# A two-layer decoder trunk on one core: four operands laid out by the host instead of turned over by transposes

## The chip, the core and the metric

The kernel runs on one core of a Trainium2 chip. Its engines are TensorE (PE, with PEld for its weight loads), VectorE (DVE), ScalarE (ACT), GpSimd (POOL) and SyncE (SP), which only issues transfers; POOL and ACT issue transfers too. Matmuls write into eight banks of PSUM, each 128 partitions by 512 f32; everything else lives in SBUF. The metric is the device time of one execution in microseconds, the median of three runs. What the host does to lay out the inputs before the launch is not part of it.

## The reference

Two layers work on `x` of 512 positions by 1024. In each layer, with an rmsnorm ahead of and behind every sub-layer:

```
z = h @ w_in                               # split among three mixers
w = where(tril, sgu_w, 0)                  # sgu_w (4, 128, 128), indices h, t, s
s = einsum('hts,bnshd->bnthd', w, v) + sgu_b.T     # sgu_b (4, 128)
A = u * s                                  # spatial gating, chunks of 128
B = retention(...)                         # 6 heads of 64
C = forgetting_attention(...)              # 6 heads of 64
x += rmsnorm(concat(A, B, C) @ w_o)
g = h @ w_gate                             # 1024 -> 4096
conv = conv_b + sum_j shift(g, j) * conv_w[j]      # conv_w (3, 4096)
x += rmsnorm((gelu(conv) * (h @ w_up)) @ w_down)
x += rmsnorm((p[i] @ w_ple_proj) * sigmoid(rmsnorm(x) @ w_ple_gate))   # p[i] (512, 256)
```

All inputs are float32. `sgu_w`, `sgu_b`, `conv_w`, `conv_b` and `p` are the ones that the change touches.

## The kernel before, in words

**Data.** Large weights are laid out by the host (`packed`, L507) so that a transfer reads long rows. In the kernel they are split into a coarse part and a remainder (tiles in fp32r), and a product is a sum of products of parts. The 4096 columns of the feed-forward network are worked off in 32 blocks of 128. For one block `gate_up` (L1285) runs 84 matmuls of 128x128 by 128x256 (`alpha`, `beta`, `gamma` are their banks; `wsa`, `wsb`, `wg` are weights prepared by DVE and ACT from a loaded `graw`), and from block 4 on a share of the down projection (`dn`) stands between them. The gate half then goes through a convolution of three taps: ACT makes `cv` from `gs` with a tap and the bias as per-partition scalars, and DVE adds the two other taps. These scalars stand in `cw`, 128 partitions by 4 by 32.

**Stages.** For each layer: `mixers` (L965), `out_proj` (L1244), `ffn` (L1274), and the gated embedding of `p` at the layer's end, whose product `p @ w_ple_proj` is made much earlier (`embed_operands` from L1376, `embed`). The spatial gating is in `mixers` at L997: it waits for gate values `av`, and its results `oa` are turned over again into the concatenated operand by `cps` transposes. Attention's blocks are `pe` (the exponentials, on ACT), turned over by `tps`, then `fet`. `rr`, `rm` and `mix` belong to the retention's rotary and its products. The program's start (L1471 to L1512) runs 16 idle bf16 matmuls, then `embed_operands(0, (0,), True)`, that is, half of layer 0's embedding product, then the first chunk of `x` and its norm (`junk` is what ACT's squares write, `h` the normed chunk, `hps` its transposes).

**Where transposes stand that the change concerns.** `sgu_w[l]` is loaded with position t on the partitions into `sguw`, masked there by POOL, turned over by four `wtps` transposes into one bank, and copied by ACT to `wT`. `sgu_b[l]` is loaded as 4 rows into `sgub`, turned over (`sbps`), and copied by DVE to `bT`. `conv_w` and `conv_b` are loaded as 128 rows of 128 into `cpar`, turned over (`cpps`), and copied by DVE to `cw` (L1275 to L1281). `p[l]` is loaded in two halves into `pr` with positions on the partitions, turned over by eight `pps` transposes, and each bank is split by ACT and DVE to `pT`. This is done twice for layer 0 (once for each half of the output columns) and once for layer 1.

**What sets the order.** Nothing is issued where it is written. Class `Plan` (L51) records every operation with its tiles, and `issue` (L252, the call itself in L452) replays them by a list scheduler: each engine takes, of the operations whose inputs its cost model holds ready, the earliest in the program. An operation may start ahead of its place only by a window counted in operations (`AHEAD`, L62). A tile from a pool waits until one of the pool's buffers is free: `sguw`, `sgub`, `cpar`, `pr`, and the mixers' `rr`, `sq`, `oa`, as well as the network's `gs`, `us`, `cv`, are all tiles of one pool of twelve buffers of 128x512 (`wk`, L565). So an operation less in one place can shift others before and behind it. On the chip, each engine runs its own list in that fixed order and waits at its head. Since every instruction is issued in L452, all rows of the profile name that line, and an operation is known by its tiles.

Of the kernel before, what the change touches and what calls it, by code (L numbers as in the profile page):

```python
# [33 lines left out]
ALU = mybir.AluOpType  # L34
AX = mybir.AxisListType

P = 128
D = 1024
S = 512
NCH = 4  # L40
# [466 lines left out]
def packed(w):  # L507

    def turned(m):
        n = block(m.shape[-1])  # L510
        m = m.reshape(*m.shape[:-1], -1, n // 2, 2)
        return m.swapaxes(-1, -2).reshape(*m.shape[:-3], -1)

    def rows(m, order=None):

        m = turned(m).reshape(-1, P, m.shape[-1])
        return (m if order is None else m[list(order)]).transpose(1, 0, 2)

    def blocks(m):

        return m.reshape(KB, P, -1, P).transpose(2, 1, 0, 3).reshape(-1, P, KB * P)

    r = {}
    r["uv"] = [rows(m[:, C_U:C_U + 512]) for m in w["w_in"]]
    r["rv"] = [rows(m[:, C_RV:C_RV + 384]) for m in w["w_in"]]
    r["fv"] = [rows(m[:, C_FV:C_FV + 390]) for m in w["w_in"]]
    def pairs(g, u):
        g, u = (blocks(m).reshape(-1, P, 2, 512) for m in (g, u))
        return np.stack([u[:, :, 1], u[:, :, 0], g[:, :, 0], g[:, :, 1]], 2)

    r["rg"] = [blocks(m[:, C_RG + 2 * P:C_RG + 3 * P])[0] for m in w["w_in"]]
    r["fm"] = [pairs(*(np.concatenate([m[:, p[i]:p[i] + P] for p in PAIRS], 1) for i in range(2))) for m in w["w_in"]]
    r["gu"] = [pairs(g, u) for g, u in zip(w["w_gate"], w["w_up"])]
    r["dn"] = [turned(m).reshape(8, 4, P, 2, 512).transpose(0, 3, 2, 1, 4) for m in w["w_down"]]
    r["wo"] = [np.stack([rows(m[:, c:c + 512], O_ORDER) for c in (0, 512)]) for m in w["w_o"]]
    r["pg"] = [np.stack([rows(m[:, c:c + 512]) for c in (0, 512)]) for m in w["w_ple_gate"]]
    r["pe"] = [rows(m) for m in w["w_ple_proj"]]
    return {k: np.ascontiguousarray(np.stack(v)) for k, v in r.items()}


def body(ctx, tc, a, out):
    nc = tc.nc
    plan = Plan(tc)
# [18 lines left out]
    def bank(name="ps"):  # L562
        return ppt([P, 512], F32, tag="ps", name=name, bufs=8)

    def wk(name, shape=(P, 512), dt=F32):  # L565
        return kpt(list(shape), dt, tag="wk", name=name, bufs=12)
# [90 lines left out]
    def split(dst_hi, dst_lo, src):  # L657
        A.copy(dst_hi, src)
        V.tensor_tensor(out=dst_lo, in0=src, in1=dst_hi.bitcast(F32), op=ALU.subtract)
# [305 lines left out]
    def mixers(l, hT, uv, ready):  # L965
# [5 lines left out]
        wT = m2[:, 1536:2048]  # L971
# [24 lines left out]

        def gating():  # L997

            wn = wk("sguw")
            SY.dma_start(out=wn.rearrange("p (h s) -> p h s", h=4), in_=a["sgu_w"][l].rearrange("h t s -> t h s"))  # L1000
            G.affine_select(out=wn, in_=wn, pattern=[[0, 4], [-1, P]], compare_op=ALU.is_ge, fill=0.0, base=0, channel_multiplier=1)
            ps = bank("wtps")
            for h in range(4):
                T.transpose(ps[:, h * P:(h + 1) * P], wn[:, h * P:(h + 1) * P], ident)
            A.copy(wT, ps)
            sb = wk("sgub", (P, P))
            SY.dma_start(out=sb[0:4, :], in_=a["sgu_b"][l])
            ps = bank("sbps")
            T.transpose(ps[:, 0:4], sb[0:4, :], ident[0:4, 0:4])
            bT = small("bT", 4, bufs=2)  # L1010
            V.tensor_copy(bT, ps[:, 0:4])
            SY.dma_start(out=gv, in_=a["sgu_v_g"][l].rearrange("h d -> (h d)").unsqueeze(0).to_broadcast([P, 256]))
            ss = small("ss16", 16, bufs=1)
            for hf in range(2):
                sq = wk("sq")
                src = m4[:, 1024 + hf * 512:1024 + hf * 512 + 512]
                A.activation(sq, src, AF.Square, scale=0.125)
                V.tensor_reduce(out=ss[:, hf * 8:hf * 8 + 8], in_=sq.rearrange("p (g d) -> p g d", d=64), axis=AX.X, op=ALU.add)
            r16 = rstd([ss], 16)
            for c in range(NCH):  # L1020
                v3 = av[:, c, :].rearrange("p (h d) -> p h d", h=4)
                V.tensor_tensor(out=v3, in0=v3, in1=r16[:, c * 4:c * 4 + 4].unsqueeze(2).to_broadcast([P, 4, 64]), op=ALU.mult)
                V.tensor_tensor(out=av[:, c, :], in0=av[:, c, :], in1=gv, op=ALU.mult)
            oa = [wk("oa") for _ in range(2)]
            pss = [bank("sps") for _ in range(2)]
            with plan.together():
                for h in range(4):
                    T.matmul(pss[h // 2][:, h % 2 * 256:h % 2 * 256 + 256], lhsT=wT[:, h * P:(h + 1) * P], rhs=av[:, :, h * 64:h * 64 + 64], start=True, stop=True)
            for b, ps in enumerate(pss):
                ov = oa[b].rearrange("p (c s d) -> p c s d", c=NCH, s=2)  # L1030
                for i in range(2):
                    h, hs = 2 * b + i, slice(i * 256, i * 256 + 256)
                    V.scalar_tensor_tensor(
                        out=ov[:, :, i, :], in0=ps[:, hs].rearrange("p (c d) -> p c d", c=NCH), scalar=bT[:, h:h + 1],
                        in1=au[:, :, h * 64:h * 64 + 64], op0=ALU.add, op1=ALU.mult)
            for b in range(2):
                to_concat(cc, b, oa[b])
# [166 lines left out]
        for step in STEPS.split():  # L1204
            h = int(step[1]) if len(step) > 1 else 0
# [66 lines left out]
        return emb  # L1272

    def ffn(l, hs, emb, ready, x, new, g, nxt):  # L1274
        cpar = wk("cpar")  # L1275
        SY.dma_start(out=cpar[0:96, 0:P], in_=a["conv_w"][l].rearrange("j (b f) -> (j b) f", f=P))
        SY.dma_start(out=cpar[96:128, 0:P], in_=a["conv_b"][l].rearrange("(b f) -> b f", f=P))
        ps = bank("cpps")
        T.transpose(ps[:, 0:P], cpar[:, 0:P], ident)
        cw = wpt([P, 4, 32], F32, tag="cw", name="cw", bufs=1)  # L1280
        V.tensor_copy(cw, ps[:, 0:P].rearrange("p (j b) -> p j b", j=4))  # L1281
        facc = []
        acts = {}

# [91 lines left out]
    def embed_operands(l, halves=range(2), at_once=False):  # L1376

        pT = b8("pT", (2, 2, S), F32R)
        raw = b8("eraw", (2, D))
        us = {hf: b8("ehl", (2, 2, 512), F32R) for hf in halves}  # L1380

        def weights(k):
            for hf, u in us.items():
                cs = slice(hf * 512, hf * 512 + 512)
                SY.dma_start(out=raw[:, k, cs], in_=a["w_pe"][l][:, k, cs])

        weights(0)
        prs = []
        for c2 in range(2):
            pr = wk("pr")  # L1390
            prs.append(pr.rearrange("p (c n) -> p c n", c=2))
            SY.dma_start(out=prs[c2], in_=a["p"][l, 0, c2 * 256:c2 * 256 + 256, :].rearrange("(c p) n -> p c n", p=P))
            if not c2:
                weights(1)
        for c2, prv in enumerate(prs):
            for k in range(2):
                ps = bank("pps")
                for c in range(2):
                    T.transpose(ps[:, c * P:(c + 1) * P], prv[:, c, k * P:(k + 1) * P], ident)
                ts = slice(c2 * 256, c2 * 256 + 256)  # L1400
                split(pT[:, 0, k, ts], pT[:, 1, k, ts], ps[:, 0:256])
                if not c2:
                    for hf, u in us.items():
                        split(u[:, 0, k, :], u[:, 1, k, :], raw[:, k, hf * 512:hf * 512 + 512])
            if at_once:
                embed(l, pT, us, range(1, NCH) if c2 else range(1))
                plan.fence(not c2)
        return pT, us

    def embed(l, pT, us, chunks=range(NCH)):  # L1410

        for hf, u in us.items():
            cs = slice(hf * 512, hf * 512 + 512)
            e = b8("e", (NCH, 512))
            for c in chunks:
                ps = bank("eps")
                ts = slice(c * P, c * P + P)
                for k in range(2):
                    mm3(ps, lambda i: pT[:, i, k, ts], lambda i: u[:, i, k, :], k == 0, k == 1)
                A.copy(e[:, c, :], ps)  # L1420
                SY.dma_start(out=ed[l][:, c, cs], in_=e[:, c, :])
# [77 lines left out]
    parts = []  # L1499
# [16 lines left out]
    for l in range(DEPTH):  # L1516
# [17 lines left out]
    plan.issue()  # L1534


_INS = ["x", "p", "positions", "sgu_v_g", "sgu_w", "sgu_b", "fox_b_f", "conv_w", "conv_b", "mix_pre_g", "mix_post_g",
        "ffn_pre_g", "ffn_post_g", "ple_pre_g", "ple_post_g"]


# [17 lines left out]
```

## Time and profile before

| | us |
|---|---|
| median of three runs | 1526.82 (1526.79 to 1529.71) |
| the profiled execution | 1528.62 |
| span of its profile | 1526.9 |

The span is what the profile's clock covers, from the first to the last recorded instruction; the execution's own time is 1.7 us longer.

| engine | busy us | share of the span | instructions |
|---|---|---|---|
| PE | 1496.3 | 98% | 10554 |
| PEld | 1383.6 | 91% | 10554 |
| DVE | 1216.7 | 80% | 2036 |
| ACT | 888.9 | 58% | 1501 |
| POOL | 194.3 | 13% | 233 |

In a timeline, a row gives the start (us from the span's start), the time from the first start to the last end, the engine, the line, the operation, `out<-in` by the program's names, shapes and the number of instructions run together in the row; in brackets stands idle time ahead of it and what ended it. A row of the waits gives the engine's waiting tile, the one it waited for, the sum in us, how often, and the longest. A row of the groups gives the sum in us and the mean in ns, and behind the bar the idle time ahead. A row of the windows gives the stretch and its length, the busy us of PE, PEld, DVE, ACT and POOL with instructions in brackets, the granted clock of TensorE (1.00 is full speed), the share of the transfer engines and their GB/s.

### The profile page before, as it was taken

Reading aid. Unit: us, or ns where it says so; the run is one execution under the profiler, and the core shown is the slowest. Engines: PE = TensorE matmul, PEld = TensorE weight load, DVE = VectorE, ACT = ScalarE, POOL = GpSimd, SP = SyncE. Lnnn points to the kernel's source line nnn. Section 1 sums busy time; section 2 is a strip of 40 time slices with the busy share of each in tenths; the row PEclk is TensorE's granted clock in tenths of the full one; section 3 lists DMA queues with packets and bytes.
Section 4 is the critical chain, followed back from the end, with each engine's and each line's share of the span. In section 5 each row is a group of like instructions: output and inputs, shape, how many; then the busy total and the mean of one; then the engine's idle time right before and its main releaser. Section 6 shows DMA issues by size and latency. Waiting matters only on the chain.

```text
span 1526.9 us, 26942 instructions
## 1 busy us (share of the span) xinstructions
PE 1496.3 (98%) x10554; PEld 1383.6 (91%) x10554; DVE 1216.7 (80%) x2036; ACT 888.9 (58%) x1501; POOL 194.3 (13%) x233
## 2 busy tenths in 40 slices
PE   8999999999999999999999999999999999999997
PEld 6998888899999999998889887799999999999987
DVE  6888969978778777768797779799688778778685
ACT  8557647755555545545575565587655555455462
POOL 1111102111101111100120102121101011011010
PEclk9999999999999999999999999999999999999999
DMA  9445619735646646556573355295545565465541
GB/s 335 88 135 122 209 52 280 189 90 146 173 90 175 150 117 173 146 155 245 190 197 99 92 146 182 68 334 130 146 117 153 163 149 130 123 174 139 212 174 70
DMA packets 87879, 239.02 MB, mean 157 GB/s; under 512 B 10036, under 2 KB 18364, under 8 KB 87752
## 3 DMA queue, kind: packets, MB, share of 16 engines
q1 hardware_dynamic: 64856, 195.81, 37.6%
q0 software_dynamic: 22464, 40.90, 17.0%
q8 instruction: 83, 1.36, 0.4%
q10 hardware_dynamic: 432, 0.59, 0.1%
q14 instruction: 44, 0.36, 0.1%
HBM read 219.94 MB, written 17.33 MB: 155 GB/s over the span
## 4 chain that ended last, share of the span: by engine, by line
PE 74%; DVE 8%; DMA 5%; ACT 5%; issue 5%; POOL 1%; SPq 0%; POOLq 0%; DVEq 0%; ACTq 0%
PE beta L452 20%; PE dn L452 19%; PE ps L452 13%; PE gamma L452 11%; PE alpha L452 5%; DMA graw<-in_w_gu_dram 3%; DMA traw<-in_w_dn_dram 2%; PE wo L452 1%; ACT rr L452 1%; PE hps L452 1%; DVE cv L452 1%; PE tps L452 1%; PE ops L452 1%; ACT junk L452 1%; POOL y L452 1%
## 5 line engine op out<-in xcount | busy, mean ns | idle before, releaser
L452 PE MATMUL dn<-thl,act 128*128 128x512 f32 x1536 | 351.7, 380 | 0.0
L452 PEld LDWEIGHTS dn<-thl,act 128*128 128x128 f32 x1536 | 281.8, 189 | 35.0
L452 POOL DMA_DIRECT2D graw<-in_w_gu_dram x128 | 112.1, 908 | 733.4 <-DVE wg L452 232.0
L452 PE MATMUL ps<-thl,hT 128*128 128x512 f32 (+3 forms) x984 | 198.7, 358 | 2.5 <-ACT hT L452 2.4
L452 PEld LDWEIGHTS ps<-thl,hT 128*128 128x128 f32 x984 | 171.6, 189 | 19.5 <-ACT hT L452 2.9
L452 DVE TENSOR_TENSOR thl<-traw,thl 128x1024 fp32r<-128x1024 f32 (+3 forms) x124 | 141.8, 1152 | 13.4 <-ACT thl L452 13.3
L452 ACT CAST thl<-traw 128x1024 fp32r<-128x1024 f32 (+3 forms) x124 | 121.2, 995 | 21.2 <-PE dn L452 9.2
L452 PEld LDWEIGHTS beta<-hh,wu 128*128 128x128 f32 x936 | 123.2, 191 | 7.2 <-DVE us L452 1.4
L452 PE MATMUL beta<-hh,wu 128*128 128x256 f32 x936 | 126.2, 275 | 1.0 <-DVE us L452 0.9
L452 PE MATMUL beta<-hh,wsa 128*128 128x256 f32 x936 | 120.6, 277 | 6.1 <-ACT gs L452 3.2
L452 PE MATMUL gamma<-hhd,wsa 128*128 128x256 f32 x936 | 120.8, 277 | 0.9 <-ACT wsa L452 0.8
L452 PEld LDWEIGHTS beta<-hh,wsa 128*128 128x128 f32 x936 | 111.4, 192 | 9.2 <-ACT gs L452 4.4
L452 PE MATMUL beta<-hh,wsb 128*128 128x256 f32 x936 | 118.0, 276 | 0.1
L452 DVE TENSOR_TENSOR graw<-graw 128x512 f32<-128x512 f32 x156 | 106.7, 684 | 10.4 <-DMA graw<-in_w_gu_dram 7.9
L452 PEld LDWEIGHTS gamma<-hhd,wsa 128*128 128x128 f32 x936 | 113.1, 194 | 1.3 <-ACT wsa L452 1.0
L452 PEld LDWEIGHTS beta<-hh,wsb 128*128 128x128 f32 x936 | 111.2, 193 | 0.3 <-ACT gs L452 0.3
L452 ACT CAST wsa<-graw 128x1024 fp32r<-128x1024 f32 x78 | 82.0, 1051 | 43.2 <-PE gamma L452 24.7
L452 DVE TENSOR_TENSOR wg<-graw,wg 128x1024 fp32r<-128x1024 f32 x78 | 95.1, 1219 | 13.0 <-ACT wg L452 12.8
L452 DVE TENSOR_TENSOR wsa<-graw,wsa 128x1024 fp32r<-128x1024 f32 x78 | 95.1, 1219 | 10.0 <-ACT wsa L452 9.9
L452 DVE SCALAR_TENSOR_TENSOR cv<-gs,cw,cv 128x511 f32<-128x511 f32 (+1 forms) x128 | 95.0, 743 | 8.5 <-ACT cv L452 8.2
L452 DVE TENSOR_TENSOR wsb<-graw,wsb 128x1024 fp32r<-128x1024 f32 x78 | 95.0, 1218 | 6.6 <-ACT wsb L452 5.9
L452 ACT CAST wg<-graw 128x1024 fp32r<-128x1024 f32 x78 | 82.1, 1053 | 30.5 <-PE gamma L452 13.2
(225 smaller groups left out, 2620.6 us busy)
## 6 DMA issues: line engine op xcount, KB each, us to landing
graw<-in_w_gu_dram SPq DMA_DIRECT2D x128, 512.0 KB
graw<-in_w_gu_dram POOLq DMA_DIRECT2D x128, 256.0 KB, 5.4
traw<-in_w_dn_dram SPq DMA_DIRECT2D x64, 512.0 KB
x<-x SPq DMA_DIRECT2D x40, 512.0 KB
graw<-in_w_fm_dram SPq DMA_DIRECT2D x28, 512.0 KB
traw<-in_w_wo_dram SPq DMA_DIRECT2D x16, 512.0 KB
traw<-in_w_pg_dram SPq DMA_DIRECT2D x16, 512.0 KB
graw<-in_w_fm_dram POOLq DMA_DIRECT2D x28, 256.0 KB, 5.1
```

The lines of the kernel that those rows point to most:

```text
L452: made = o[1](*[self.map(v) for v in o[2]], **{k: self.map(v) for k, v in o[3].items()})
```

## The change

The host lays out four more operands in `packed`: the taps and the bias as `cv` (128, 4, 32), `sgu_w` as `sw` with s ahead of h and t, `sgu_b` turned over as `sb`, and `p` turned over as `pt` (128, 2, 512). The kernel loads them where the transposed copies stood. `sgu_w` goes straight into `wT` and POOL masks it there, with the pattern turned over. `bT` and `cw` are transfers. The splits to `pT` read the loaded `pr` in SBUF, no longer a bank of PSUM. In the program's start `p` comes in four transfers of 128 KB, positions 0 to 255 first, where two of 256 KB stood.

```diff
+    r["cv"] = [np.concatenate([m, b[None]]).reshape(4, -1, P).transpose(2, 0, 1) for m, b in zip(w["conv_w"], w["conv_b"])]
+    r["sw"] = [m.transpose(2, 0, 1) for m in w["sgu_w"]]
+    r["sb"] = [m.T for m in w["sgu_b"]]
+    r["pt"] = [m[0].T.reshape(2, P, S).transpose(1, 0, 2) for m in w["p"]]
...
         def gating():
-            wn = wk("sguw")
-            SY.dma_start(out=wn.rearrange("p (h s) -> p h s", h=4), in_=a["sgu_w"][l].rearrange("h t s -> t h s"))
-            G.affine_select(out=wn, in_=wn, pattern=[[0, 4], [-1, P]], compare_op=ALU.is_ge, fill=0.0, base=0, channel_multiplier=1)
-            ps = bank("wtps")
-            for h in range(4):
-                T.transpose(ps[:, h * P:(h + 1) * P], wn[:, h * P:(h + 1) * P], ident)
-            A.copy(wT, ps)
-            sb = wk("sgub", (P, P))
-            SY.dma_start(out=sb[0:4, :], in_=a["sgu_b"][l])
-            ps = bank("sbps")
-            T.transpose(ps[:, 0:4], sb[0:4, :], ident[0:4, 0:4])
+            SY.dma_start(out=wT.rearrange("p (h t) -> p h t", h=4), in_=a["w_sw"][l])
+            G.affine_select(out=wT, in_=wT, pattern=[[0, 4], [1, P]], compare_op=ALU.is_ge, fill=0.0, base=0, channel_multiplier=-1)
             bT = small("bT", 4, bufs=2)
-            V.tensor_copy(bT, ps[:, 0:4])
+            SY.dma_start(out=bT, in_=a["w_sb"][l])
...
     def ffn(l, hs, emb, ready, x, new, g, nxt):
-        cpar = wk("cpar")
-        SY.dma_start(out=cpar[0:96, 0:P], in_=a["conv_w"][l].rearrange("j (b f) -> (j b) f", f=P))
-        SY.dma_start(out=cpar[96:128, 0:P], in_=a["conv_b"][l].rearrange("(b f) -> b f", f=P))
-        ps = bank("cpps")
-        T.transpose(ps[:, 0:P], cpar[:, 0:P], ident)
         cw = wpt([P, 4, 32], F32, tag="cw", name="cw", bufs=1)
-        V.tensor_copy(cw, ps[:, 0:P].rearrange("p (j b) -> p j b", j=4))
+        SY.dma_start(out=cw, in_=a["w_cv"][l])
...
-        weights(0)
-        prs = []
-        for c2 in range(2):
-            pr = wk("pr")
...
-        for c2, prv in enumerate(prs):
+        prs = [wk("pr") for _ in range(2)]
+
+        def rows(k, ts):
+            SY.dma_start(out=prs[k][:, ts], in_=a["w_pt"][l][:, k, ts])
+
+        parts = [slice(0, 256), slice(256, S)] if at_once else [slice(0, S)]
+        for k in range(2):
+            rows(k, parts[0])
+            weights(k)
+        for ts in parts[1:]:
             for k in range(2):
-                ps = bank("pps")
-                for c in range(2):
-                    T.transpose(ps[:, c * P:(c + 1) * P], prv[:, c, k * P:(k + 1) * P], ident)
-                ts = slice(c2 * 256, c2 * 256 + 256)
-                split(pT[:, 0, k, ts], pT[:, 1, k, ts], ps[:, 0:256])
...
+                rows(k, ts)
+        for i, ts in enumerate(parts):
+            for k in range(2):
+                split(pT[:, 0, k, ts], pT[:, 1, k, ts], prs[k][:, ts])
```

Since the list scheduler plans anew, operations also change places. Three such places follow, one for each of PE, ACT and DVE.

PE's list in layer 0's mixers, around the gating (`hT` by `fhl` are projections for attention, `tps` attention's transposes, `sps` the gating's own products, `beta` the next projection's), before:

```order
L452 MATMUL gps<-hT,fhl 128x512 x3
L452 MATMUL wtps<-k_ident,sguw 128x128
L452 MATMUL tps<-k_ident,pe 128x128 x3
L452 MATMUL wtps<-k_ident,sguw 128x128
L452 MATMUL tps<-k_ident,pe 128x128 x3
L452 MATMUL wtps<-k_ident,sguw 128x128 x2
L452 MATMUL sbps<-k_ident,sgub 128x4
L452 MATMUL beta<-hT,wg 128x256 x10
L452 MATMUL sps<-mix_312,mix_804 128x256 x4
```

The same place with the change:

```order
L452 MATMUL gps<-hT,fhl 128x512 x8
L452 MATMUL tps<-k_ident,pe 128x128 x3
L452 MATMUL gps<-hT,fhl 128x512 x5
L452 MATMUL sps<-mix_306,mix_794 128x256 x4
L452 MATMUL tps<-k_ident,pe 128x128 x3
L452 MATMUL beta<-hT,wg 128x256 x7
```

The transposes of `sguw` and `sgub` are gone, and the gating's products `sps` stand between attention's transposes, ahead of the `beta` matmuls that they followed.

ACT's list in layer 0's mixers, the difference between before (-) and the change (+); `rr` are the rotary's copies of 32 partitions, and `pe,den` the first exponentials of attention:

```order
 L452 ACTIVATE rr<-rm 32x512
 L452 COPY rr<-rm 32x512
+L452 ACTIVATE rr<-rm 32x512
+L452 COPY rr<-rm 32x512
+L452 ACTIVATE rr<-rm 32x512
+L452 COPY rr<-rm 32x512
 L452 ACTIVATE pe,den<-pe,nm 128x128 x2
-L452 ACTIVATE rr<-rm 32x512
-L452 COPY rr<-rm 32x512
-L452 ACTIVATE rr<-rm 32x512
-L452 COPY rr<-rm 32x512
-L452 ACTIVATE pe,den<-pe,nm 128x256
```

All of the `rr` copies now stand ahead of the first exponential; two pairs stood behind it.

DVE's list at layer 0's entry into the feed-forward network, around the weights `wsa` of its block 4 (the tile's number is written after its name; `graw_3034` is block 4's loaded weight), before:

```order
L452 TENSOR_TENSOR act_3382<-cv_3301,act_3382 128x512
L452 TENSOR_TENSOR gs_3082<-gamma_3326,gs_3082 128x256
L452 TENSOR_TENSOR graw_3034<-graw_3034 128x512
L452 TENSOR_TENSOR wg_3322<-graw_3237,wg_3322 128x1024
L452 SCALAR_TENSOR_TENSOR cv_3410<-gs_3082,cw_2856,cv_3410 128x511
L452 TENSOR_TENSOR graw_3034<-graw_3034 128x512
L452 SCALAR_TENSOR_TENSOR cv_3410<-gs_3082,cw_2856,cv_3410 128x510
L452 TENSOR_TENSOR wsa_3421<-graw_3034,wsa_3421 128x1024
```

The same place with the change, where block 4's weight is `graw_2990`:

```order
L452 TENSOR_TENSOR graw_2990<-graw_2990 128x512
L452 SCALAR_TENSOR_TENSOR cv_3280<-gs_3022,cw_2473,cv_3280 128x511
L452 TENSOR_TENSOR act_3174<-cv_3226,act_3174 128x512
L452 SCALAR_TENSOR_TENSOR cv_3280<-gs_3022,cw_2473,cv_3280 128x510
L452 TENSOR_TENSOR graw_2990<-graw_2990 128x512
L452 TENSOR_TENSOR wsa_3304<-graw_2990,wsa_3304 128x1024
```

In DVE's list `wsa` of block 4 stood 40 instructions behind `wsa` of block 1 and now stands 29 behind it.

More of the change, by code (lines that the diff above doesn't have):

```diff
@@ L1385, in weights @@
                 SY.dma_start(out=raw[:, k, cs], in_=a["w_pe"][l][:, k, cs])
-        weights(0)
-        prs = []
-        for c2 in range(2):
-            pr = wk("pr")
[L1391 to L1394, printed above, removed]
-        for c2, prv in enumerate(prs):
-            for k in range(2):
-                ps = bank("pps")
-                for c in range(2):
-                    T.transpose(ps[:, c * P:(c + 1) * P], prv[:, c, k * P:(k + 1) * P], ident)
-                ts = slice(c2 * 256, c2 * 256 + 256)
-                split(pT[:, 0, k, ts], pT[:, 1, k, ts], ps[:, 0:256])
-                if not c2:
+        prs = [wk("pr") for _ in range(2)]
[6 more added lines that the diff above has]
+        for ts in parts[1:]:
+            for k in range(2):
+                rows(k, ts)
+        for i, ts in enumerate(parts):
+            for k in range(2):
+                split(pT[:, 0, k, ts], pT[:, 1, k, ts], prs[k][:, ts])
+                if not i:
                     for hf, u in us.items():
@@ L1405, in embed_operands @@
             if at_once:
-                embed(l, pT, us, range(1, NCH) if c2 else range(1))
-                plan.fence(not c2)
+                embed(l, pT, us, range(1, NCH) if i else range(1))
+                plan.fence(not i)
         return pT, us
@@ L1534, in body @@
     plan.issue()
-_INS = ["x", "p", "positions", "sgu_v_g", "sgu_w", "sgu_b", "fox_b_f", "conv_w", "conv_b", "mix_pre_g", "mix_post_g",
+_INS = ["x", "positions", "sgu_v_g", "fox_b_f", "mix_pre_g", "mix_post_g",
         "ffn_pre_g", "ffn_post_g", "ple_pre_g", "ple_post_g"]
@@ L1546 @@
     given = {n: np.ascontiguousarray(inputs[n]) for n in _INS}
-    given.update({"w_" + n: v for n, v in packed({k: np.asarray(inputs[k]) for k in ("w_in", "w_o", "w_gate", "w_up", "w_down", "w_ple_gate", "w_ple_proj")}).items()})
+    given.update({"w_" + n: v for n, v in packed({k: np.asarray(inputs[k]) for k in ("w_in", "w_o", "w_gate", "w_up", "w_down", "w_ple_gate", "w_ple_proj", "conv_w", "conv_b", "sgu_w", "sgu_b", "p")}).items()})
     given.update({"c_" + n: v for n, v in constants().items()})
```

## The prediction

> **What bounds the kernel now.** I read the page's totals first, then the waits of TensorE, then the timeline at the places where the transposes and the largest waits stand.
>
> ```profile
> span 1526.9 us, 26942 instructions
> PE 1496.3 (98%) x10554; PEld 1383.6 (91%) x10554; DVE 1216.7 (80%) x2036; ACT 888.9 (58%) x1501; POOL 194.3 (13%) x233
> ```
>
> TensorE is busy for 98% of the span, so what leaves its stream leaves the time, unless a wait fills the hole. The waits of PE between 31 and 1519 us (tile, the tile waited for, sum in us, times, longest), the first three and the last of 16 rows, which come to 17 us:
>
> ```profile
> PE beta L452 <- ACT gs L452: 3.2, 5, 1.4
> PE tps L452 <- DVE fet L452: 2.9, 2, 1.5
> PE beta L452 <- DVE wsa L452: 2.6, 2, 2.2
> ...
> PE gamma L452 <- ACT fqk L452: 0.2, 1, 0.2
> ```
>
> No wait is above 3.2 us in sum. So the kernel is bound by TensorE's stream, with small waits and, at 292 us, a slow clock. A different order can move single microseconds; the change itself can take out only what its instructions cost. The sum below is made against the profiled execution, 1528.62 us (span 1526.9 and 1.7 around it). That is 1.8 above the median, 1526.82 (1526.79 to 1529.71), so I carry the difference in us over to the median. About 0.2%, or 3.05 us, is what a measurement here can tell from no change: below 1523.77 is faster, above 1529.87 slower.
>
> **Term 1: the transposes outside the start.**
>
> ```profile
> L452 PE MATMUL pps<-k_ident,pr 128*128 128x128 f32 x24 | 3.8, 274 | 0.1
> L452 PE MATMUL wtps<-k_ident,sguw 128*128 128x128 f32 x8 | 1.5, 273 | 0.0
> L452 PE MATMUL cpps<-k_ident,cpar 128*128 128x128 f32 x2 | 0.5, 272 | 0.0
> L452 PE MATMUL sbps<-k_ident,sgub 4*128 4x4 f32 x2 | 0.4, 219 | 0.0
> 135.62 1.04 PE L452 MATMUL tps<-k_ident,pe 128*128 128x128 f32 x8
> 136.50 1.04 PE L452 MATMUL cps<-k_ident,oa 128*128 128x128 f32 x8
> ```
>
> These are 36 instructions of about 0.273 us each by their own records. But records overlap in a pipeline: of the last two rows, each eight transposes, the first starts at 135.62 and the second at 136.50, so one costs the stream 0.88 / 8 = 0.11 us. The same can be seen in the first row: 24 transposes were busy for 3.8 us, 0.16 each, with the ends of groups counted whole.
>
> Of the 34 large ones, 8 belong to the start. The other 26 cost 26 x 0.109 = 2.8 us; the two 4x4 ones I put at 0.22 each, their own record. **Term 1 is -3.3 us** (bounds: -2.9 with the small ones at 0.02 each, -7.5 with all at their records). Nothing hides it: the matmuls behind them are ready.
>
> [...]
>
> **What else the change touches, at nothing.** The transfers and the mask that replace the transposes stand in these rows of before (queues SP and POOL, layer 0's mixers):
>
> ```profile
> 84.07 7.09 DMA sguw<-in_sgu_w_dram
> 84.78 0.44 SPq L452 DMA_DIRECT2D sgub<-in_sgu_b_dram  x1
> 91.30 0.88 POOL L452 TENSOR_SCALAR_AFFINE_SELECT sguw<-sguw 128x512 f32<-128x512 f32 x1 [14.39 <-DMA sguw<-in_sgu_w_dram]
> 91.71 0.34 SPq L452 DMA_DIRECT2D fraw<-in_w_rg_dram  x1
> 95.67 2.93 POOL L452 TENSOR_TENSOR y<-vh,minus_half 128x16 f32<-128x16 f32 x1 [3.49 <-DVE vh L452]
> 100.96 0.93 POOL L452 DMA_DIRECT2D graw<-in_w_fm_dram  x1 [2.36 <-PE sps L452]
> 133.90 1.89 PE L452 MATMUL sps<-mix,mix 128*128 128x256 f32 x8
> 134.96 1.74 DVE L452 SCALAR_TENSOR_TENSOR oa<-sps,bT,mix 128x256 f32<-128x256 f32 x4 [0.44 <-PE sps L452]
> ...
> L452 SPq DMA_DIRECT2D cpar<-in_conv_w_dram x2: 327/328/328, 192.5 to 953.3; - x2
> L452 ACT ACTIVATE cv<-gs,cw x64: 802/817/839, 263.7 to 1444.8; 128x512 f32<-128x512 f32 x64
> ```
>
> The load of `wT` now stands behind that of `fraw`, so it goes out at about 92.1; with the 7.1 us of its predecessor it lands at 99.2, and the mask ends near 100.1. POOL's list has it behind `y`, which ends at 98.6, and ahead of the load at 100.96, which thus isn't held up. The gating's products `sps` need it at 133.90, some 3 us earlier in the new order: cover 30 us, and behind it a late mask would cost its lateness. `bT`, loaded near 85, isn't used until 134.96. `cw`, loaded where `cpar` was (the last rows: first at 192.5, first use at 263.7), has 70 us, and the splits of `pT` read as many elements from SBUF as they read from PSUM. I put all of that at 0. ACT loses two copies to `wT` and DVE four small ones; neither engine is the bound there.
>
> **Term 2: the start.**
>
> ```profile
> 7.01 0.63 PE L452 MATMUL pps<-k_ident,pr 128*128 128x128 f32 x4
> 9.77 0.63 ACT L452 ACTIVATE junk<-x 128x512 bf16<-128x512 f32 x1 [1.02 <-DMA x<-in_x_dram]
> 11.43 0.65 ACT L452 CAST pT<-pps 128x256 fp32r<-128x256 f32 x2
> 11.95 0.65 ACT L452 ACTIVATE junk<-x 128x512 bf16<-128x512 f32 x1
> 15.22 0.63 PE L452 MATMUL hps<-k_ident,h 128*128 128x128 f32 x4 [0.49 <-DVE h L452]
> ```
>
> PE loses eight transposes (0.87 us) and its hand-over to ACT. But the next thing it needs, `h`, hangs on ACT's two passes over `x`, and the first of these waits for a transfer until 9.77. What comes free is the pair of `pT` casts between the two passes: with the change they stand ahead of the first one, in ACT's 1.02 us of waiting. That is 0.5 us (11.43 to 11.95). Against it, SP issues two transfers more ahead of `x`. Bounds are -1.1 (transposes and the wait for `pT`) and +0.4 (the load of `x` late by two issues of 0.44, as at 84.78 for `sgub`, less the cast). I take **-0.5 us**, from the cast's row.
>
> **Term 3: the wait in layer 0's mixers.**
>
> ```profile
> 102.69 0.63 ACT L452 ACTIVATE rr<-rm 32x512 f32<-32x512 f32 x1 [1.23 <-DVE rm L452]
> 105.26 0.69 DVE L452 TENSOR_TENSOR rm<-rm,mix 128x512 f32<-128x512 f32 x1 [1.58 <-ACT rr L452]
> 106.81 0.33 PE L452 MATMUL tps<-k_ident,pe 128*128 128x128 f32 x1 [1.51 <-DVE fet L452]
> ```
>
> PE stands 1.51 us for `fet`, which DVE makes behind an `rm` that waited for ACT's `rr`. `rr` takes a buffer of the pool of twelve, of which `sguw` and `sgub` held two from 84 to 132 us; now they hold none, and the order puts all `rr` copies ahead of the exponentials. Bounds 0 and -1.5; I take the middle, **-0.8 us**.
>
> **Term 4: the stall at layer 0's entry into the feed-forward network.** Timeline rows, then two windows (length, busy of PE, PEld, DVE, ACT, POOL, granted clock, transfers' share and GB/s):
>
> ```profile
> 261.69 1.23 DVE L452 TENSOR_TENSOR wsa<-graw,wsa 128x1024 fp32r<-128x1024 f32 x1
> 289.47 1.21 DVE L452 TENSOR_TENSOR wsa<-graw,wsa 128x1024 fp32r<-128x1024 f32 x1
> 290.73 1.53 PE L452 MATMUL beta<-hh,wsa 128*128 128x256 f32 x10 [2.25 <-DVE wsa L452]
> 292.06 2.77 PE L452 MATMUL gamma<-hhd,wsa 128*128 128x256 f32 x12
> 296.26 1.50 PE L452 MATMUL gamma<-hb,wsb 128*128 128x256 f32 x12
> 261.69:289.47 27.78, 26.17 (x226) 25.34 (x224) 27.78 (x41) 23.03 (x37) 3.83 (x5) 1.00 0.76 213
> 291.83:295.24 3.41, 3.41 (x18) 3.41 (x17) 3.41 (x6) 2.11 (x6) 0.11 (x1) 0.50 0.99 237
> ```
>
> DVE is busy for all of the 27.78 us between the starts of block 1's and block 4's `wsa`, 40 instructions, 0.69 each. PE has to wait 2.25 us for the last, and then runs 3.41 us at half clock, in which 12 matmuls take 2.77 rather than 1.50 us: some 16 matmuls at twice 0.11, 1.6 us more. The stall costs 3.9 us in all. In the new order 29 instructions stand between the two, 29 x 0.69 = 20 us, which would bring `wsa` some 7 us earlier. That isn't the whole of it: what it passed is now behind it and needed soon after. The `act` that stood 33 behind block 1's `wsa` stands 34 behind it, and the two `thl`, weights of the down projection, go from 29 and 32 to 36 and 39, 7 x 0.69 = 5 us later, so `dn` could be the next to wait. Bounds 0 and -3.9. I take **-2.5 us**, near the case in which the wait shrinks below where the clock drops and a wait of about a microsecond is left.
>
> [...]
>
> **Term 5: waits that the new order makes.** The whole program is planned anew, and layer 1's mixers and entry are rearranged too. No row of before shows such a wait. Below it is bounded by 0, or a gain as large as term 3's; above by several of 1.5. I charge one wait like that at 106.81: **+1.6 us** with its hand-over.
>
> The sum: -3.3 - 0.5 - 0.8 - 2.5 + 1.6 = **-5.5 us**, that is 1523.1 for an execution like the profiled one, 1521.3 for the median.
>
> **The rivals.**
> - Only the transposes go; waits come and go in equal parts. -3.3 - 0.5 = -3.8, 1523.0. For it: the 17 us of waits are of 16 kinds, none above 3.2, so no single one is there to be won. Against: term 4 has an order that says otherwise.
> - More is gained: 3.3 + 1.1 + 1.5 + 3.9 = 9.8, 1517.0. Against it: each term at its end.
> - A transpose costs its whole record, 0.273: 36 x 0.27 = 9.8, about 1517. Against it: the step of 0.11. It would also hold if every transpose broke the rhythm of the matmuls around it, which its rows do not show.
> - The change's gain is given back by waits on DVE and transfers: DVE is full for 27.78 of 27.78 us at an entry, so it has no room for a worse order there. Two to three such waits leave 1524 to 1529.8, say 1526.8.
> - Slower: the cold clock. The price of one stall like that at 290.73 is 3.9 us. If the new order makes two of them at the entries into the feed-forward networks, and the old one stays: -3.8 + 7.8 = +4.0, 1530.8. It decides from the point where PE waits about 2 us: 1.51 at 106.81 left the clock up, 2.25 did not. For it: one such stall stands there before, and DVE is full. Against: layer 0's new order brings `wsa` forward.
> - That it does not do what it says: the transposes are plainly out of PE's list (36 less), so I give this none.
>
> **How the numbers follow.** Forecast 1521.3 (1518.5 to 1523) 42%; only the transposes 22%; larger 7%; whole records 3%; given back 18%; slower 8%. Of the second, a third falls above 1523.77. Faster: 42 + 15 + 7 + 3 = 67%; the same: 7 + 17 = 24%; slower: 8 and 1 of the given back, 9%. The range goes from 1517.0 (the larger case and whole records) to 1528.5, which takes in most of the given back and leaves out the slower case; that is some 8 in 10.
>
> **What would show it.** PE has 10518 instructions and no row of `pps`, `wtps`, `sbps`, `cpps`. Term 2: the first `hps` starts between 14.2 and 15. Term 3: no wait of over 1 us for `fet` near 105. Term 4: clock 1.00 in the stretch from 280 to 300, and a wait for `wsa` under 1.3 us. Term 5: among the waits of PE, one or two new ones of 1 to 2 us, with the sum of all within 2 us of 17. The prediction is wrong if a stretch at half clock stands at another place, if the waits' sum rises by more than 2 us, or if PE's busy time falls by 9 us and not by 5.

## The result, and the profile after

| | before | after |
|---|---|---|
| median of 4 runs each, us | 1528.26 (1526.79 to 1531.70) | 1518.45 (1515.81 to 1520.67) |
| ratio, 95% interval | | 0.9933 (0.9911 to 0.9955) |
| profiled execution, us | 1528.62 | 1520.67 |
| span, us | 1526.9 | 1518.9 |

The kernel is 9.8 us faster by the medians. Forecast were 5.5. The profiled execution after is the slowest of its four, which matters below. The page of the kernel after (span; busy time and instructions of each engine):

```profile
span 1518.9 us, 26820 instructions
PE 1492.3 (98%) x10518; PEld 1380.7 (91%) x10518; DVE 1213.5 (80%) x2028; ACT 887.5 (58%) x1495; POOL 195.4 (13%) x233
```

TensorE has 36 instructions less, and its busy time fell by 4.0 us (1496.3 to 1492.3), not by 9; in a second profile of this kernel, which lacks two stretches at half clock that this one has (mean granted clock 0.998 against 0.996), it is 1489.5. What is left of the gain must be waiting, so the next view is the windows, laid over the same stages: stretch and length, busy us of PE, PEld, DVE, ACT and POOL, granted clock, transfers' share, GB/s. A stage's waiting is its length less PE's busy time. Before:

```profile
100.00:240.00 140.00, 136.74 (x936) 117.60 (x933) 119.06 (x304) 87.41 (x175) 18.54 (x24) 1.00 0.43 123
240.00:320.00 80.00, 76.44 (x595) 73.17 (x594) 75.65 (x110) 58.36 (x95) 14.33 (x16) 0.98 0.73 205
...
820.00:950.00 130.00, 125.22 (x961) 111.20 (x959) 106.87 (x265) 78.66 (x147) 16.22 (x18) 1.00 0.50 147
950.00:1055.00 105.00, 102.53 (x704) 91.95 (x703) 94.17 (x166) 73.64 (x136) 21.48 (x26) 1.00 0.62 180
```

After, with the ends moved to where TensorE stands at about the same matmuls:

```profile
100.00:238.00 138.00, 136.58 (x933) 117.36 (x932) 120.17 (x306) 88.00 (x174) 18.78 (x25) 1.00 0.43 129
238.00:315.00 77.00, 74.46 (x593) 71.27 (x592) 73.13 (x109) 57.34 (x95) 15.54 (x17) 1.00 0.79 223
...
816.00:945.00 129.00, 125.88 (x973) 112.54 (x972) 105.33 (x263) 78.45 (x147) 16.40 (x18) 1.00 0.51 151
945.00:1048.00 103.00, 101.57 (x697) 91.26 (x696) 92.91 (x163) 72.84 (x135) 21.16 (x24) 1.00 0.62 182
```

| stage | PE idle before | after | less |
|---|---|---|---|
| layer 0, mixers and output projection | 3.26 | 1.42 | 1.8 |
| layer 0, entry into the feed-forward network | 3.56 | 2.54 | 1.0, and 1.6 of half clock |
| layer 1, mixers | 4.78 | 3.12 | 1.7 |
| layer 1, output projection and entry | 2.47 | 1.43 | 1.0 |

That is 7.1 us of stalls in four places, two of which the prediction never looked at, and with the transposes' 1.4 to 3.2 (measured below) it makes 8.5 to 10.3. Against that, the other five stages idle 1.0 us more in sum, the first `hps` comes 0.9 us later, and there is half clock (0.50) from 18.60 to 22.01 and from 656.89 to 660.30: this profile is 8.0 us shorter than the one before, not 9.8. The waits of PE after, between 31 and 1511 us, the first three and the last of 14 rows, which come to 12.5 us:

```profile
PE hps L452 <- DVE h L452: 2.5, 6, 0.6
PE beta L452 <- ACT gs L452: 2.1, 4, 1.1
PE gamma L452 <- ACT us L452: 2.1, 2, 1.8
...
PE beta L452 <- ACT fqk L452: 0.2, 1, 0.2
```

The rows `tps <- DVE fet` (2.9 us, two waits) and `beta <- DVE wsa` (2.6) are gone from the list. The longest wait is now 1.8, and it belongs to a late transfer. The timeline of TensorE shows it:

```profile
16.16 0.66 PE L452 MATMUL hps<-k_ident,h 128*128 128x128 f32 x4 [1.43 <-DVE h L452]
269.75 0.71 PE L452 MATMUL beta<-hh,wsb 128*128 128x256 f32 x4 [0.67 <-DVE wsb L452]
283.23 1.60 PE L452 MATMUL beta<-hh,wu 128*128 128x256 f32 x12 [0.81 <-DVE us L452]
655.65 1.83 PE L452 MATMUL gamma<-hb,wsb 128*128 128x256 f32 x12 [1.83 <-ACT us L452]
```

and the window behind it the price, a clock of 0.50:

```profile
656.89:660.30 3.41, 3.41 (x12) 2.77 (x11) 3.38 (x7) 1.75 (x2) 0.00 (x0) 0.50 0.28 73
```

The start got no better (first `hps` at 16.16, before at 15.22). In place of the stall of 2.25 us at 290.73, with its half clock, stand two waits of 0.67 and 0.81 at full clock. At 655.65 a weight landed late (DVE stood 2.62 us for the transfer of `graw`) and ACT, held at a cast of it, gave `us` late; with the half clock behind it this one costs about 3.6 us, since the 22 matmuls of `dn` that follow take 6.41 us where 22 of them take 4.91 in the kernel before. The kernel before has a wait of that kind too (1.42 us at 410.5, without half clock). They differ from run to run, as the repeats below show, and are probably one reason why runs of one kernel lie some 5 us apart.

### The profile page after: what moved, and what is told of

It reads as the page before. It is cut to its first block, busy times and chain, and to the rows that moved or that the text cites. A ratio compares the mean times of both kernels' runs of the same rounds, so it can differ in the third digit from the quotient of the medians.

```text
span 1518.9 us, 26820 instructions
## 1 busy us (share of the span) xinstructions
PE 1492.3 (98%) x10518; PEld 1380.7 (91%) x10518; DVE 1213.5 (80%) x2028; ACT 887.5 (58%) x1495; POOL 195.4 (13%) x233
## 3 DMA queue, kind: packets, MB, share of 16 engines
q8 instruction: 82, 1.34, 0.4%
## 4 chain that ended last, share of the span: by engine, by line
PE 79%; DVE 8%; DMA 5%; ACT 4%; issue 2%; POOL 1%; SPq 0%; POOLq 0%; ACTq 0%; DVEq 0%
PE beta L452 23%; PE dn L452 20%; PE ps L452 12%; PE gamma L452 12%; PE alpha L452 5%; DMA graw<-in_w_gu_dram 3%; PE wo L452 2%; PE hps L452 1%; DMA traw<-in_w_dn_dram 1%; PE sps L452 1%; PE tps L452 1%; DMA graw<-in_w_fm_dram 1%; PE ops L452 1%; ACT junk L452 1%; DVE x L452 1%
## 5 line engine op out<-in xcount | busy, mean ns | idle before, releaser
L452 DVE TENSOR_TENSOR facc<-dn,facc 128x512 f32<-128x512 f32 x112 | 76.6, 686 | 36.8 <-PE dn L452 36.6
```

What stands on the lines that cost most here:

```text
L452: made = o[1](*[self.map(v) for v in o[2]], **{k: self.map(v) for k, v in o[3].items()})
```

## The experiments

Two theories stood at first. **A**: a transpose costs its step in TensorE's stream, about 0.1 us, and the larger part of the gain is the new order's. **B**: a transpose costs its whole record of 0.27 us, 9.8 us for 36, and the order brings nothing. B gives the measured time by itself, so it had to be tried first. Each kernel was timed against the kernel before on the same chip; that one's medians were 1528.60, 1528.81 and 1528.83 in the three sets.

### The transposes left out, everything else in the old order

```diff
-            made = o[1](*[self.map(v) for v in o[2]], ...)
+            args, kw = o[2], o[3]
+            if i in self.swap:
+                if self.swap[i] is None:
+                    continue
+                args, kw = self.swap[i]
+            made = o[1](*[self.map(v) for v in args], ...)
```

A transpose has `None` there, and the copy or split behind it the loaded tile. The planner still sees the old operations, so all engines keep their lists and the buffers their holders.

> The operands come laid out by the host and the 36 transposes are left out, but everything else is issued in the order of the kernel before, buffers too. Theory A (a transpose costs its step in TensorE's stream, 0.11 us, and the rest of the gain of about 10 us is the new order's): 3 to 5 us less than before, so about 1523 to 1525; the wait for fet near 106.8 and the stall at half clock near 291 are still there, each within 0.5 us of before. Theory B (a transpose costs its whole record, 0.27 us, and the order brings nothing): 9 to 10 us less, about 1518.

Measured: 1530.11 (11 runs, 1527.60 to 1532.45), ratio 1.0015 (1.0006 to 1.0024). **Both theories missed the time: without a new order the change gains nothing, and is slower by a hair.** The waits are where A had them:

```profile
108.00 0.33 PE L466 MATMUL tps<-k_ident,pe 128*128 128x128 f32 x1 [1.50 <-DVE fet L466]
...
290.24 1.60 PE L466 MATMUL beta<-hh,wsa 128*128 128x256 f32 x10 [2.25 <-DVE wsa L466]
```

(L466 is the issuing line of this kernel.) In the windows PE's idle time is 3.5 and 3.4 us in layer 0's two stages (before 3.3 and 3.6), 5.5 and 3.0 in layer 1's (before 4.8 and 2.5), and 4.0 rather than 2.2 in layer 1's network, where in the profiled run TensorE waited 1.98 us at 1160.91, behind a late load, and the 12 matmuls after it took 2.27 us (12 of that size took 1.60 behind the wait at 655.79 of the changed kernel's second profile). So part of the transposes' time came back as waiting. The profiled run also stood 1.2 us behind at the first wait for `fet` (108.00 against 106.81), 0.6 of it from the start, where the first `hps` came at 15.83 rather than 15.22. How much of all this is this list's and how much chance is not settled. It is settled that B is out.

### The new order, with 36 transposes put back

```diff
             pss = [bank("sps") for _ in range(2)]
+            plan.more[pss[0].tensor.name] = 6
...
                 ps = bank("eps")
+                plan.more[ps.tensor.name] = 2 if len(us) == 1 else 1
```

> The changed kernel in its own order, with 36 transposes of the identity put back on TensorE's list where the old ones fed: six ahead of each layer's gating products, the others ahead of the products of p; their banks are overwritten. Nothing else waits for them. Together with fixed_order it separates order and transposes. Theory A (order and transposes add up): the changed kernel's time plus 36 x 0.11 = 4 us, 6 us below before. Theory B (the order alone makes the difference, and the 4 us of transposes fall into waits that are there anyway): within 1.5 us of the changed kernel, 10 us below before. If the old transposes were the cause, it would come back to within 2 us of before.

Measured: 1519.73 (6 runs), ratio 0.9940 (0.9923 to 0.9956). With TensorE's old number of instructions, 10554, the new order keeps 9 of its 11 us. Against the changed kernel in another set (1517.23 and 0.9931, below) 36 transposes cost 2.5 us by the medians and 1.4 by the ratios, 0.04 to 0.07 each. That lies between the two theories of its expectation (4 us, or under 1.5), and since the intervals of the two ratios overlap, this run does not tell A's step from none. What it does show is that the order carries the gain.

### What a transpose costs, by many of them

```diff
             ps = bank("dn")
+            plan.more[ps.tensor.name] = 2
```

The first kernel for this added none, since its condition met no operation; it ran as the changed kernel and counts as a repeat of it.

> The changed kernel with two more 128x128 transposes of the identity ahead of each of the 128 groups of down-projection matmuls (256 in all), into the bank that the group then overwrites. Theory A (cost is the step): 256 x 0.11 = 28 us more than the changed kernel, each record still near 0.27 us. Theory B (cost is the record): 256 x 0.273 = 70 us more.

Measured: 1519.52 (2 runs), ratio 0.9945 (0.9928 to 0.9962), 10518 instructions on PE.

> What extra_transposes was to measure, with the condition mended (that kernel's list held none of them and it ran as the changed kernel): the changed kernel with two more 128x128 transposes of the identity ahead of each of the 128 groups of down-projection matmuls, 256 in all. Theory A (cost is the step in the stream): 256 x 0.11 = 28 us more than the changed kernel, each record near 0.27 us. Theory B (cost is the record): 70 us more.

Measured: 1541.66 (4 runs), ratio 1.0082 (1.0062 to 1.0101); the changed kernel's was 0.9931. That is 24.4 us more for 256 by the medians, 0.095 each. The group of the added ones (busy us, mean ns) and their place in the timeline:

```profile
L455 PE MATMUL dn<-k_ident 128*128 128x128 f32 x256 | 48.9, 273 | 0.0
...
411.16 0.38 PE L455 MATMUL dn<-k_ident 128*128 128x128 f32 x2
411.30 2.84 PE L461 MATMUL dn<-thl,act 128*128 128x512 f32 x12
```

Each has a record of 0.273 us, and 0.14 us after the first of two the next matmul starts. So the record overlaps the next matmul's, and what one added to the time, 0.095 us, lies by the step and not by the record: A.

### The changed kernel again, and the start with two transfers

The second kernel loads `p` in the start as before, in two transfers of 256 KB, behind the first weights `eraw`:

```diff
+            prs = [wk("pr").rearrange("p (k t) -> p k t", k=2) for _ in range(2)]
...
+                SY.dma_start(out=prs[c2], in_=a["w_pt"][l][:, :, c2 * 256:c2 * 256 + 256])
```

> The changed kernel once more, for what repeats. Both theories: 8 to 11 us below before. What belongs to the program repeats in the trace within 0.3 us: no wait for fet near 105, no half clock between 280 and 300, the first hps near 16.2 and half clock at 18.6. What is a late transfer of one execution does not: the wait of 1.83 us at 655.65 for ACT us, behind a graw that landed late, with 3.41 us of half clock, and in the kernel before the wait of 1.42 us at 410.5.

> The changed kernel with one edit: in the program's start p comes in two transfers of 256 KB, as before, instead of four of 128 KB. Theory A (the two further transfers ahead of x on SP's list make SP wait for an earlier transfer to end, until 7.29 instead of 4.51, so that x's second half and the weights are late): SP issues x's second half near 4.9, the first hps starts at 14.2 to 14.9 instead of 16.16, no stretch of half clock at 18.6, and the time is 1.5 to 3 us below the changed kernel's. Theory B (x's landing is set by the bytes that the transfers share, which are the same): the first hps stays at 15.8 to 16.3 and the time is the changed kernel's.

Measured: the changed kernel 1517.23 (6 runs), 0.9931 (0.9918 to 0.9944); two transfers 1517.10 (5 runs), 0.9929 (0.9917 to 0.9940). They are the same. SP did issue the second half of `x` at 4.95 rather than 7.66, as theory A said, but then the larger load of `p` came late:

```profile
8.39 0.71 ACT L452 CAST pT<-pr 128x256 fp32r<-128x256 f32 x2 [3.38 <-DMA pr<-in_w_pt_dram]
```

and the first `hps` started at 15.33. In the three profiles of the changed program it started at 16.16, 15.66 and 14.98, with half clock at 18.6 in the first alone (mean granted clock 0.996, and 0.998 in each of the others). So my claim that the start's lateness repeats was wrong: it varies by 1.2 us between profiles of one program. The wait at 655 did repeat, which I had put down to one execution: 2.15 us in the second profile, 1.24 in the third, 0.66 with two transfers. In the first profile a late load stands behind it; its length varies from one profile to the next.

### Only the gating part, and the same with its two buffers held

The first kernel takes over only `sgu_w` and `sgu_b`. The second does so as well, but keeps them in two of the twelve buffers until the gating has read them (shown against the first):

```diff
+            wn = wk("sguw")
+            SY.dma_start(out=wn.rearrange("p (h t) -> p h t", h=4), in_=a["w_sw"][l])
...
+            bT = wk("sgub", (P, P))
...
-                    T.matmul(..., lhsT=wT[:, h * P:(h + 1) * P], ...)
+                    T.matmul(..., lhsT=wn[:, h * P:(h + 1) * P], ...)
```

> The kernel before with only sgu_w and sgu_b laid out by the host: 10 of the 36 transposes and the two held buffers go, and the program is planned anew. If the two buffers of sguw and sgub cause the waits for fet near 106.8 and 853.9, both waits go here (2.8 us) with about 1.3 us of transposes, and the time is about 4 us below before; the stall near 291 may stay. If those waits come from the order as a whole, they stay over 1 us, and the time is within 2 us of before.

> As gating_only, without the 10 transposes and planned anew, but sgu_w and sgu_b stay in the two buffers of the pool of twelve until the gating's products and sums have read them. Theory A (the freed buffers let rr go earlier): the waits for fet near 106 and 853 are back, 1.3 to 1.5 us each, and the time is 3 us or more above gating_only's 1517.2. Theory B (the buffers don't matter, the new order does): the waits stay gone and the time is within 2 us of gating_only's.

Measured: the gating part alone 1517.22 (4 runs), 0.9924 (0.9901 to 0.9947), as fast as the whole change with 10 of the 36 transposes removed; with the buffers held 1527.07 (10 runs), 0.9986 (0.9973 to 0.9999). **The same removal of transposes, with the two buffers still held, loses nearly all of the gain.** Both waits for `fet` are gone in the first kernel and back in the second, at nearly before's lengths (1.51 and 1.35):

```profile
107.86 0.33 PE L452 MATMUL tps<-k_ident,pe 128*128 128x128 f32 x1 [1.51 <-DVE fet L452]
...
861.80 0.33 PE L452 MATMUL tps<-k_ident,pe 128*128 128x128 f32 x1 [1.34 <-DVE fet L452]
```

ACT's rows show where it starts. It makes eight pieces of `rr`. With the buffers held there is a hole behind the fourth, and the fifth waits for an `rm` of DVE. That is the operation that reads the first `rr` (`rm<-rm,rr`, 102.97 to 103.65), so the fifth piece starts only when the buffer of the first four has been read:

```profile
100.98 0.61 ACT L452 COPY rr<-rm 32x512 f32<-32x512 f32 x1
...
103.74 0.63 ACT L452 ACTIVATE rr<-rm 32x512 f32<-32x512 f32 x1 [1.24 <-DVE rm L452]
```

With the gating part alone the fifth follows on the fourth (101.16 behind 100.53), 1.5 us before that read of the first `rr` (102.65), and the last ends at 103.69 rather than 106.27:

```profile
100.53 0.61 ACT L452 COPY rr<-rm 32x512 f32<-32x512 f32 x1
101.16 0.63 ACT L452 ACTIVATE rr<-rm 32x512 f32<-32x512 f32 x1
```

The two waits are 2.9 us of the 9.9 between these kernels. The held one also has a new wait of 1.95 us near 169, and a late load of 2.86 at 537; its order differs in other places too. Its granted clock was 0.99 in the window from 100 to 240 and 0.98 in that from 240 to 320, and 1.00 in both with the gating part alone (0.996 and 0.999 over the whole profiles), so part of the 9.9 may be chance (see the clock below). That the held buffers bring back the two waits is shown; what the other 7 us hang on is not. Nor do these two waits and ten transposes explain the gating part's whole 11.6 us.

### Only p, only the taps

Each of these takes over its part of the diff and no other.

> The kernel before with only p laid out by the host: 24 of the 36 transposes go, in the start, near 214 us and in layer 1. Theory A (a transpose is worth 0.1 us of TensorE's stream and the rest is the gating part's new order): 1 to 3 us below before, 1526 to 1528, with the waits near 106.8 and 853.9 still there. Theory B (the gain goes by transposes): two thirds of it, 7 us below before.

> The kernel before with only the convolution's taps laid out by the host: 2 of the 36 transposes and a buffer at the entry into the feed-forward network go. Theory A: what happens before the first entry is as before, with the wait near 106.8; the time is within 2 us of before, unless the new order at the entries takes the stall near 291 away, which is worth up to 3.9. Theory B (the gain goes by transposes): 0.5 us.

Measured: `p` alone 1521.84 (4 runs), 0.9953 (0.9935 to 0.9970); the taps alone 1525.15 (6 runs), 0.9970 (0.9957 to 0.9982). In both, the waits for `fet` stay (1.5 and 1.3 us), as A said. With the taps alone, two transposes, the stall of 290.73 is gone, and exactly the two small waits of the changed kernel stand in its place:

```profile
271.33 0.71 PE L452 MATMUL beta<-hh,wsb 128*128 128x256 f32 x4 [0.67 <-DVE wsb L452]
...
284.80 1.60 PE L452 MATMUL beta<-hh,wu 128*128 128x256 f32 x12 [0.81 <-DVE us L452]
```

So term 4 is the taps' doing. `p` alone gained 7.0 us, the figure of theory B, though B is excluded above: 24 steps of 0.095 are 2.3 us. Its profile does not explain the rest; it was taken of the slowest of its runs (1524.77), 4.4 us behind the fastest. This stays open. The parts sum to 22 us (7.0, 3.7 and 11.6) where the whole change gives 11.4: they do not add.

### One piece of DVE's list moved, and a wider window

The first kernel is the one before, with `graw` and `wsa` of block 4 put ahead of the two `cv` steps on DVE; the second the one before with another setting of the planner.

```diff
...
+        for i in (dve[at - 2], made):
+            order.remove(i)
+            order.insert(max([order.index(first)] + [order.index(j) + 1 for j in ops[i][4]]), i)
...
-    AHEAD = {"mix": 416, ...
+    AHEAD = {"mix": 426, ...
```

> The kernel before, transposes and all, with one piece of DVE's list moved at layer 0's entry into the feed-forward network: the second graw and wsa of block 4 go ahead of the two convolution steps cv that stood among them. wsa is then ready 2 x 0.74 = 1.5 us earlier. Theory A (the stall at 290.73 costs its wait and the half clock behind it, 3.9 us): the wait falls from 2.25 to about 0.8, the stretch at half clock near 291 is gone, and TensorE is 2.5 to 3.1 us earlier from 300 us on; the time is 2 to 3 us below before. Theory B (the work passed over makes TensorE wait as long): a wait of over 1 us turns up for dn or for the next block between 292 and 310, and the time is within 1 us of before.

> The kernel before with all its work, and the planner's window for the mixers at 426 operations instead of 416, so that it looks ten operations further ahead; ten is about what the gating part takes out of each layer's list. Theory A (any new order moves the time by microseconds, and the change drew a good one): the time differs from before by more than 3 us, up or down, with other waits in the same stages. Theory B (the gain comes from what the change frees): within 2 us of before, the waits near 106.8 and 853.9 still there.

Measured: the move 1528.65 (12 runs), 1.0002 (0.9989 to 1.0014); the window 1529.24 (10 runs), 1.0003 (0.9994 to 1.0013). The move shows theory B of its expectation in the timeline of TensorE:

```profile
288.91 1.38 PE L460 MATMUL beta<-hh,wsa 128*128 128x256 f32 x10 [1.06 <-DVE wsa L460]
290.13 1.50 PE L460 MATMUL gamma<-hhd,wsa 128*128 128x256 f32 x12
293.76 1.60 PE L460 MATMUL beta<-hh,wsb 128*128 128x256 f32 x12 [2.13 <-ACT gs L460]
```

The wait for `wsa` shrank from 2.25 to 1.06, but TensorE then waited 2.13 us for ACT's `gs`, one group further. On ACT `gs` stands behind `cv`, two casts of `thl` and one of `act`. It starts at 293.34 (293.20 before), and ACT stood only 0.67 us for the `cv` that was passed over. In the kernel before, TensorE came to this place later, out of the stall and the half clock, and so did not wait. The first wait had hidden the second. The wider window has both waits for `fet` still (1.34 and 1.51) and the median of before, as its theory B said: this one order that is merely different does not give the gain; others were not tried.

## Why the prediction was right, and where it was not

- **The direction and the bound were right.** TensorE's stream sets the time (busy for 98% of the span before and after), 36 instructions left it, and the range held the time. The gain was 9.8, not 5.5.
- **Term 1** (-3.3): its 26 large transposes at 0.04 to 0.07 (put back) or 0.095 (256 added) are 1.0 to 2.5 us, where it put 2.8, so it was somewhat too large. Its bound of 0.02 for a small one stands in no row: the matmul behind `sbps` starts 0.15 us after it (132.53 and 132.68, before). "Nothing hides it" did not hold: with the old order kept, no gain was left at all.
- **Term 2** (-0.5): not seen. The start varies by 1.2 us from profile to profile; the freed casts are within that.
- **Term 3** (-0.8): right in mechanism, half its size. The buffers of `sguw` and `sgub` held `rr` back, and the whole wait of 1.51 us went.
- **Term 4** (-2.5): about right in size. PE's idle time in the stage fell by 1.0 and 1.6 us of half clock went, 2.6 in sum. The cause is the taps' part, and `wsa`'s place on DVE alone does not do it: moved alone, it passed the wait on to `gs`.
- **Term 5** (+1.6) is the step that was wrong: "I charge one wait like that at 106.81". It was put in for a new wait, since no row of layer 1 was read. But layer 1 runs the same gating with the same two buffers. Its own wait for `fet` was in the trace of before:

```profile
853.86 0.33 PE L452 MATMUL tps<-k_ident,pe 128*128 128x128 f32 x1 [1.35 <-DVE fet L452]
```

The waits row said "2.9, 2, 1.5", two waits, and the prediction priced one. Layer 1's two stages lost 2.7 us of idle time where 1.6 were added. Together that is 4.3 us, as much as lies between forecast and result (9.8 less 5.5). That they agree so closely is partly luck: term 1 was put too large and term 2 did not show, term 3 was too small, and the new wait that term 5 charges did come, at 655.65 with half clock, in the profiled run.

- **Its signs.** As said, PE has 10518 instructions, the clock is 1.00 from 280 to 300, and the waits for `fet` are gone. The waits' sum was to stay within 2 us of 17 and fell to 12.5. One sign of being wrong came true: half clock at another place, at 18.6 and 656.9 (0.50 at both). It is in the first profile and at neither place in the second, so it marks a run and not the mechanism.
- **Of the rivals**, "a transpose costs its whole record" gave the right time (1517) for a wrong reason; the added transposes exclude it. "More is gained" (1517.0, each term at its end) was the nearer one, though only term 3 reached its end, and the waits of layer 1, which it did not count, made up for the others.

## What to carry to other kernels

In a program that a list scheduler orders, price an instruction on the bound engine by its step, not its record (here 0.095 us and 0.273), and then ask what the operation held: two buffers held for 48 us cost more here (2.9 us of waits in the two layers) than the ten transposes that held them (under 1 us). If a wait stands twice in the row of waits, price it in both layers. To separate order from work, keep the plan and leave the work out, and keep the plan and put the work back; removing parts one at a time plans each anew, and such gains do not add.

## What the runs showed of the hardware

**The clock fell after some waits of about 2 us and stayed up after others as long.** TensorE fell to 0.50 for 3.41 us after waits of 1.83 (655.65, changed kernel) and 2.25 us (290.73, before). It did not after 2.15 us at 655.79 in the second profile of the same changed kernel (1.00 from 655.79 to 662), nor after 2.26 at 290.15 with the gating part alone, whose windows right behind that wait show full clock:

```profile
290.00:293.41 3.41, 3.09 (x25) 2.90 (x26) 3.41 (x6) 3.41 (x7) 0.00 (x0) 1.00 0.95 257
293.41:297.00 3.59, 3.59 (x30) 3.46 (x29) 3.59 (x7) 1.40 (x3) 1.76 (x2) 1.00 1.08 297
```

So the same wait costs 2.3 us or 3.9, and the length of the wait alone does not decide it, though the prediction had it so ("about 2 us"): between 1.83 and 2.26 us the clock fell in one run and stayed up in another.

The traces of the kernel before and of the change show what went with it there. Before, half clock begins at 291.83 and, in the last 3 us, at 1524.04; with the change at 18.60, 656.89 and 1513.63. The stretches that end within a run last 3.41 us each, and the distances between the starts within a run are whole multiples of that: 1232.21 us is 361 times 3.413, 638.29 is 187 times and 856.74 is 251 times. Counted in steps of this length on those starts, from 5 us on, half clock followed each step at full clock in which TensorE idled for 1.83 us or more: 2.25 (288.41 to 291.83) and the whole step (1520.62 to 1524.04) before, 1.95 (15.18 to 18.60), 1.83 (653.48 to 656.89) and 2.52 (1510.22 to 1513.63) after. The largest idle time in a step that left the clock up is 1.59 (1517.21 to 1520.62, before).

That is two profiles. How much TensorE idled in a longer window does not decide it: from 820 to 950 it idled 5.43 us at a granted clock of 0.99 with `p` alone, and 5.46 us at 1.00 in the old order without transposes. Why the clock stayed up after the 2.15 and the 2.26 us no run shows.

**SP waited, by the view of its waits, for a transfer that was not its own.** In the changed kernel's start SP stood 2.9 us, until 7.29, ahead of its eighth transfer, and the view names `gain`, which ACT's queue had loaded:

```profile
SPq L452 <- DMA gain<-in_mix_pre_g_dram: 2.9, 1, 2.9
```

With two transfers fewer ahead it issued the second half of `x` 2.7 us earlier. So splitting loads finer delayed a later issue here, though the time stayed the same. Why SP waits for that load no run shows.
